# A gather's weighted sums move to TensorE, and two recurrences to VectorE, in a two-layer diffusion trunk

## The chip, the cores and the metric

One core of one Trainium2 chip runs the whole program in one launch. The metric is the device time of one execution in microseconds (us). TensorE multiplies matrices, VectorE and ScalarE work element by element, GpSimd runs small vector operations and issues the indirect DMAs, and SyncE issues the other DMAs. In the rows below they are PE (PEld for its weight loads), DVE, ACT, POOL and SP.

## The reference, cut to what matters

```python
for layer in range(2):                       # latent x: 512 tokens, context xc: 256 tokens, width 1024
    y, yc = token_mixer(h, hc, ...)          # attention + long convolution + S5 scan, gated
    x = x + g1 * y
    x = x + g2 * peer_ffn(modulated norm of x, ...)
    if layer == 0:                           # the context is needed by layer 1 only
        xc = xc + mc[2] * yc
        xc = xc + mc[5] * peer_ffn(modulated norm of xc, ...)

def s5_scan(...):      h[t] = abar * h[t-1] + bu[t]          # complex, forward and backward

def peer_ffn(x, ...):                        # per token: 8 heads x 16 experts of 16384
    expert, gate = top-k of query-key scores
    act = gelu(einsum('btd,bthkd->bthk', x, u_tab[expert]))
    return einsum('bthk,bthkd->btd', gate * act, v_tab[expert])
```

## The kernel before, in words

The program writes its work as generators, called chains here. `weave` (L115 and on) runs several chains at once: each chain has a clock, each `yield` adds its cost (2.6 where none is given) times the chain's factor, and the chain whose clock is lowest goes next. A chain that waits for a mark is held, and its clock is raised to that of the chain that goes on. So a larger factor gives a chain a smaller share, and the factors decide the order in which instructions are written for all engines; each engine then runs its own queue in about that order.

The stages, in time, are these. **Stage A** is layer 0's mixer for latent and context. **Stage B** weaves five chains: layer 0's context mixer (`ctx_rest`), followed at the mark `c1` by `ctx_side` (the context's norm, its scores, and the choice of experts by `pick` for its two tiles of 128 tokens); `peer_u`, which multiplies all 512 latent tokens with 128 slabs of the U table; `side` (from `aside`: S5 and convolution tables for layer 1, the mark `pg`, then the latent's `scores`, four `pick`s and four `table`s of gates, and the mark `tabs`); `gather`; and layer 1's modulation (`mods`). **Stage C** is `peer_v`: 128 slabs of the V table for the latent, while `gather` goes on. **Stage D** is layer 1's mixer; then come layer 1's PEER stages.

`peer_gather` treats a context tile in two rounds of 128 indirect DMAs of 128 rows x 1024 numbers (512 KB each) into the four buffers `gx`. The first round fetches rows of U, and VectorE takes the product with the tokens and its sum (L1198). The second fetches rows of V, and VectorE adds each, weighted, to the result (L170). Round by round it goes tile 0 U, tile 0 V, tile 1 U, tile 1 V. It starts when the experts of a tile are chosen and the buffers `gx` exist; those are opened by `side` after the first `pick` or `table` that ends behind `c1`. In stage B `gather` has the factor 1.69 and ends its turn at `tabs`; the rest runs in stage C with the factor 1.5.

`s5_scan` runs the recurrence of the S5 branch: after `s5_drive` has filled Z (matrix products, copied out by ScalarE at L536), 32 steps for the context and 63 for the latent, four small operations each, on GpSimd, in each layer. `merge` and `merge_lat` gather three gated branches; one addition of each runs on GpSimd.

## Time and profile before

| | us |
|---|---|
| median of 3 runs | 5619.02 |
| lowest, highest | 5601.35, 5627.83 |
| the profiled execution, its own time | 5622.82 |
| its span, first to last instruction | 5621.0 |

Stage boundaries are read from the first and the last instruction on a tile: `pu` belongs to `peer_u` and starts at 973 us, `pa` belongs to `peer_v` and starts at 2572 us, and the chain of layer 1's mixer begins after 3432 us. A row of the view by stretches gives, for each engine, the time in which it was busy and the count of its instructions, and then the clock that TensorE was granted (1.00 is 2.4 GHz, and in each moment it is 1.2 or 2.4), the mean busy share of the 16 DMA engines, and the rate of all transfers. A matmul's recorded time is longer than the spacing of two matmuls, since they are pipelined; the spacing is what a sum of many takes.

### The profile page before, as it was taken

The page shows a single profiled execution, that of the slowest core. Times are in us where ns is not written, and L with a number is a line of the kernel's source. Part 1 is how long each engine was busy: PE and PEld are TensorE (multiplying, and loading weights), DVE is VectorE, ACT ScalarE, POOL GpSimd, SP SyncE. Part 2 cuts the span into 40 slices and gives each one's busy share as a digit, 9 for nine tenths or more (in the row PEclk, how much of TensorE's full clock was granted, in tenths as well). Part 3 has the DMA queues.
Part 4 walks back from the last instruction along what each step waited for, and adds up shares of the span by engine and source line. Part 5 has one row for each costly group of instructions (what it writes and reads, how often), then busy time and mean ns, then how long its engine had stood idle before and what let it go on. Part 6 is the DMA issues. An engine that isn't in the chain of part 4 may idle for free.

```text
span 5621.0 us, 72399 instructions
## 1 busy us (share of the span) xinstructions
PE 4884.9 (87%) x25801; PEld 4022.3 (72%) x25801; DVE 3723.0 (66%) x7594; ACT 1757.1 (31%) x2651; POOL 1480.0 (26%) x1626
## 2 busy tenths in 40 slices
PE   6898878878997889998888887999789899999887
PEld 5676547648986767786676766876578889897775
DVE  5643426654489999995776776544353989877777
ACT  3231514314442222332222223324233333333332
POOL 0003500000002334442444442406000111244443
PEclk8899989889999999999999988999899999999998
DMA  6557335666656889898999997563344576889997
GB/s 206 193 185 260 110 95 187 195 193 195 186 174 200 293 285 321 307 338 311 326 322 308 329 310 243 187 207 101 113 145 153 199 241 233 286 316 322 319 326 267
DMA packets 641793, 1333.38 MB, mean 237 GB/s; under 512 B 56437, under 2 KB 342390, under 8 KB 626328
## 3 DMA queue, kind: packets, MB, share of 16 engines
q1 hardware_dynamic: 522776, 871.53, 47.3%
q0 software_dynamic: 118656, 457.23, 23.0%
q8 instruction: 203, 3.33, 0.2%
q14 instruction: 158, 1.29, 0.1%
HBM read 1147.01 MB, written 181.49 MB: 236 GB/s over the span
## 4 chain that ended last, share of the span: by engine, by line
PE 24%; issue 14%; DVE 12%; DMA 11%; POOL 5%; ACT 1%; SPq 0%; DVEq 0%; POOLq 0%; ACTq 0%
PE pa L181 6%; PE two L181 4%; PE ps L181 4%; PE pu L181 4%; POOL gx L1185 4%; DMA gx<-in_peer_v_dram,t 3%; DVE t L170 2%; DMA gt<-t 2%; PE px L181 2%; PE pf L181 2%; PE pm L181 2%; DVE wl L160 2%; DMA va<-t 1%; DMA t<-ge 1%; DVE xl L160 1%
## 5 line engine op out<-in xcount | busy, mean ns | idle before, releaser
L160 DVE TENSOR_TENSOR wl<-w,wh 128x1024 fp32r<-128x1024 f32 (+1 forms) x550 | 638.9, 1163 | 581.2 <-ACT wh L176 574.7
L176 ACT CAST wh<-w 128x1024 fp32r<-128x1024 f32 (+1 forms) x550 | 545.9, 993 | 1499.9 <-PE pu L181 398.6
L1185 POOL DMA_INDIRECT gx<-in_peer_un_dram,t x384 | 533.3, 1389 | 1595.0 <-DVE t L1198 769.3
L181 PE MATMUL pa<-xl,vwh 128*128 128x512 f32 x1664 | 674.8, 406 | 163.9 <-DVE xl L160 163.7
L1185 POOL DMA_INDIRECT gx<-in_peer_v_dram,t x384 | 592.8, 1544 | 745.3 <-DVE t L170 642.7
L181 PE MATMUL pu<-t,wh 128*128 128x512 f32 x2048 | 661.8, 405 | 31.3 <-ACT ua L173 22.7
L181 PE MATMUL pa<-xh,vwh 128*128 128x512 f32 x1664 | 665.8, 401 | 18.3 <-ACT vwh L176 17.7
L181 PE MATMUL pa<-xh,vwl 128*128 128x512 f32 x1664 | 669.8, 403 | 5.4 <-DVE vwl L160 5.3
L181 PE MATMUL pm<-t,wh 128*128 128x384 f32 (+1 forms) x2432 | 579.4, 324 | 6.9 <-ACT wh L176 6.9
L170 DVE SCALAR_TENSOR_TENSOR t<-gx,t,t 128x1024 f32<-128x1024 f32 x381 | 487.2, 1279 | 52.4 <-DMA gx<-in_peer_v_dram,t 50.8
L181 PEld LDWEIGHTS pa<-xl,vwh 128*128 128x128 f32 x1664 | 324.9, 195 | 248.6 <-DVE xl L160 180.9
L1198 DVE CUSTOM_DVE_ANT_0 gx<-gx,t 128x1024 f32<-128x1024 f32 x384 | 462.6, 1218 | 55.0 <-DMA gx<-in_peer_un_dram,t 54.2
L181 PEld LDWEIGHTS pu<-t,wh 128*128 128x128 f32 x2048 | 391.0, 195 | 114.8 <-ACT ua L173 27.1
L181 PE MATMUL pu<-t,wl 128*128 128x512 f32 x1024 | 415.2, 406 | 57.7 <-DVE wl L160 57.7
L181 PEld LDWEIGHTS pm<-t,wh 128*128 128x128 f32 x2432 | 425.7, 193 | 15.6 <-ACT wh L176 10.0
L181 PE MATMUL pm<-t,wl 128*128 128x384 f32 (+1 forms) x1216 | 393.1, 324 | 34.8 <-DVE wl L160 34.8
L181 PEld LDWEIGHTS pa<-xh,vwh 128*128 128x128 f32 x1664 | 323.7, 195 | 88.5 <-ACT vwh L176 18.6
L181 PEld LDWEIGHTS pa<-xh,vwl 128*128 128x128 f32 x1664 | 325.2, 195 | 76.3 <-DVE vwl L160 8.3
L176 ACT CAST vwh<-gt 128x512 fp32r<-128x512 f32 (+1 forms) x256 | 145.1, 567 | 730.4 <-PE pa L181 589.4
L176 ACT CAST xh<-x 128x1024 fp32r<-128x1024 f32 x256 | 268.5, 1049 | 320.2 <-DMA x<-in_peer_v_dram 269.1
L160 DVE TENSOR_TENSOR gt<-va,gt 128x512 f32<-128x512 f32 (+1 forms) x256 | 152.2, 620 | 289.4 <-DMA gt<-t 205.0
L160 DVE TENSOR_TENSOR xl<-x,xh 128x1024 fp32r<-128x1024 f32 x256 | 311.9, 1218 | 6.3 <-ACT xh L176 6.3
(372 smaller groups left out, 9147.0 us busy)
## 6 DMA issues: line engine op xcount, KB each, us to landing
w<-in_peer_u_dram SPq DMA_DIRECT2D x256, 512.0 KB
x<-in_peer_v_dram SPq DMA_DIRECT2D x256, 512.0 KB
w<-in_in_w_dram SPq DMA_DIRECT2D x128, 512.0 KB
t<-ge SPq DMA_DIRECT2D x56, 1024.0 KB
gt<-t SPq DMA_DIRECT2D x112, 512.0 KB
w<-in_mod_w_dram SPq DMA_DIRECT2D x96, 512.0 KB
dft<-in_dft_dram POOLq DMA_DIRECT2D x32, 1024.0 KB
t<-ua SPq DMA_DIRECT2D x128, 256.0 KB
```

What stands on the lines that cost most here:

```text
L160: return (e or self.nc.vector).tensor_tensor(out=out, in0=a, in1=b, op=op)
L170: self.nc.vector.scalar_tensor_tensor(out=out, in0=a, scalar=s, in1=b, op0=op0, op1=op1)
L176: self.nc.scalar.copy(h, x)
L181: self.nc.tensor.matmul(out, l, r, start=start, stop=stop)
L1185: self.nc.gpsimd.indirect_dma_start(out=g, out_offset=None, in_=src, in_offset=bass.IndirectOffsetOnAxis(ap=ids[:, k:k + 1], axis=0))
L1198: self.nc.vector.tensor_tensor_reduce(out=g, in0=g, in1=x, scale=1.0, scalar=0.0, op0=OP.mult, op1=OP.add, accum_out=dot[:, c:c + 1])
```

## The change

Five edits. The recurrences of `s5_scan` are issued on VectorE, and every step of them yields 1.5 (before, every fourth yielded 0.5). The additions of `merge` and `merge_lat` go to VectorE. For context tile 0 the gather stops after the U round, with the mark `dot`; the V round is done by a new function `summed` at the end of `ctx_side`, in stage B: 128 rows are gathered for 4 tokens x 32 slots at a time and summed by TensorE, with the weights set into a block matrix `z` of 32 columns. `gather` in stage C gets the factor 3.0 in place of 1.5. And `side` gets the factor 1.3 in place of 0.8 until `pg` or `c1`, so 0.6 of its pace beside the context's mixer.

```diff
-        e = nc.gpsimd
+        e = nc.vector
...
-            if i % 4 == 3:
-                yield 0.5
+            yield 1.5
...
-                            self.tt(mf[:, n], mf[:, n], g, OP.add, self.nc.gpsimd)
+                            self.tt(mf[:, n], mf[:, n], g, OP.add)
...
-                                self.tt(mf, mf, g, OP.add, nc.gpsimd)
+                                self.tt(mf, mf, g, OP.add)
...
+    def summed(self, pool, src, ids, w, lane):
...
+        p = self.bank(lane)
+        f = self.t(pool, [128, 128], tag="gi", bufs=1)
+        nc.vector.tensor_copy(f, ids)
+        nc.tensor.transpose(p[:, 0:128], f, self.ident)
+        nc.tensor.transpose(p[:, 128:256], w, self.ident)
+        it = self.t(pool, [128, 128], I32, tag="git", bufs=1)
+        nc.vector.tensor_copy(it, p[:, 0:128])
+        wt = self.t(pool, [128, 4, 32], tag="gi", bufs=1)
+        nc.vector.tensor_copy(wt.rearrange("p g s -> p (g s)"), p[:, 128:256])
+        acc = [self.bank(lane) for _ in range(2)]
+        lag, made = 8 - 4, []
+        for n in range(128 + lag):
+            if n < 128:
+                t = 32 * (n % 4) + n // 4
+                g = self.t(pool, [128, D], tag="gv", bufs=8)
+                nc.gpsimd.indirect_dma_start(out=g, out_offset=None, in_=src,
+                                             in_offset=bass.IndirectOffsetOnAxis(ap=it[:, t:t + 1], axis=0))
+                made.append(g)
+            if n % 4 == (lag - 1) % 4:
+                s = (n - lag - 3) // 4
+                if s >= 0:
+                    if s % 4 == 0:
+                        z = self.t(pool, [128, 4, 4, 32], tag="gz", bufs=2)
+                        nc.vector.memset(z, 0.0)
+                        nc.vector.tensor_copy(z.rearrange("p g s c -> p g (s c)")[:, :, s:s + 100:33], wt[:, :, s:s + 4])
+                    rows = [made.pop(0) for _ in range(4)]
+                    one = lambda c, q: nc.tensor.matmul(acc[c][32 * q:32 * q + 32, :], z[:, q, s % 4, :], rows[q][:, c * 512:(c + 1) * 512],
+                                                        start=s == 0, stop=s == 31)
+                    first = one(0, 3)
+                    with self.tc.issue_after(first.ins):
+                        for c in range(2):
+                            for q in range(3, -1, -1):
+                                if c or q < 3:
+                                    one(c, q)
+                yield 6.4
+        return acc
...
+        if key:
+            self.done.add(key)
+            return
...
+            with self.pool("gv") as gv:
+                yield from until("dot", ("mods", 1))
+                x, w, ids, _ = C[0]
+                acc = yield from self.summed(gv, a["peer_v"].rearrange("l e d -> (l e) d"), ids, w[:, 2].rearrange("p h k -> p (h k)"), "m")
...
-                yield from self.peer_gather(C["gx"], 0, 1, *C[q], c1[q], lambda x: nc.sync.dma_start(c2[q], x))
+                yield from self.peer_gather(C["gx"], 0, 1, *C[q], c1[q], lambda x: nc.sync.dma_start(c2[q], x), None if q else "dot")
...
-                      (part(side, "tables"), lambda: 1.25 if "c1" in self.done else 1.23 if "pg" in self.done else 0.8, "s"),
+                      (part(side, "tables"), lambda: 1.25 if "c1" in self.done else 1.23 if "pg" in self.done else 1.3, "s"),
...
-                    weave((vl, 1.0, "m"), (gather, 1.5, "s"))
+                    weave((vl, 1.0, "m"), (gather, 3.0, "s"))
```

## Rows read from the trace of the kernel before

**Rows 1.** Stretches: us; PE, PEld, DVE, ACT, POOL busy; clock; DMA share; GB/s

```profile
0.00:960.00 960.00, 793.35 (x4594) 593.30 (x4594) 437.34 (x819) 291.47 (x484) 164.96 (x423) 0.90 0.55 176
960.00:1310.00 350.00, 273.88 (x1686) 198.57 (x1685) 203.49 (x467) 108.84 (x189) 4.82 (x9) 0.82 0.66 199
1310.00:1540.00 230.00, 226.72 (x1552) 209.62 (x1551) 95.14 (x123) 95.70 (x135) 16.07 (x19) 1.00 0.58 181
1540.00:1757.00 217.00, 203.60 (x1100) 172.31 (x1099) 188.50 (x746) 88.06 (x133) 0.00 (x0) 0.98 0.56 170
1757.00:2181.00 424.00, 352.99 (x1694) 291.48 (x1692) 392.15 (x1078) 115.49 (x169) 174.21 (x129) 0.92 0.83 293
2181.00:2555.00 374.00, 351.18 (x1753) 294.89 (x1753) 331.41 (x706) 115.52 (x172) 151.71 (x107) 0.97 0.86 308
2555.00:3432.00 877.00, 739.68 (x3063) 598.42 (x3062) 636.61 (x793) 206.85 (x259) 390.85 (x276) 0.91 0.92 320
3432.00:4300.00 868.00, 767.46 (x4305) 603.49 (x4304) 367.87 (x553) 298.94 (x493) 169.62 (x409) 0.93 0.48 154
```

**Rows 2.** Tile `my`, DVE, stage B: count, ns min/median/max, first and last start

```profile
L160 DVE TENSOR_TENSOR my<-pm,rowb x8: 417/420/425, 1499.0 to 1538.1; 128x256 f32<-128x256 f32 x8
```

**Rows 3.** Tile `gx`, 1497 to 3432 us: the first gathers of U and of V

```profile
L1185 POOL DMA_INDIRECT gx<-in_peer_un_dram,t x256: 939/1165/1996, 1757.4 to 3047.6; - x128
...
L1185 POOL DMA_INDIRECT gx<-in_peer_v_dram,t x255: 939/1154/4094, 2180.6 to 3431.7; - x128
```

**Rows 4.** Groups by line, DVE, 1757 to 2555 us: count | busy us, mean ns | idle before

```profile
L1198 DVE CUSTOM_DVE_ANT_0 gx<-gx,t 128x1024 f32<-128x1024 f32 x128 | 154.5, 1215 | 19.2 <-DMA gx<-in_peer_un_dram,t 19.1
...
L170 DVE SCALAR_TENSOR_TENSOR t<-gx,t,t 128x1024 f32<-128x1024 f32 x102 | 130.3, 1277 | 8.0 <-DMA gx<-in_peer_v_dram,t 7.4
```

**Rows 5.** DMA view, 1757 to 2555 us: bytes, and issues with count and size

```profile
DMA packets 69163, 239.47 MB, mean 300 GB/s; under 512 B 7680, under 2 KB 7680, under 8 KB 65013
...
w<-in_peer_u_dram SPq DMA_DIRECT2D x96, 512.0 KB
...
t<-ua SPq DMA_DIRECT2D x101, 256.0 KB
...
gx<-in_peer_un_dram,t POOLq DMA_INDIRECT x128
gx<-in_peer_v_dram,t POOLq DMA_INDIRECT x107
```

**Rows 6.** DMA view, stage C, 2555 to 3432 us

```profile
DMA packets 143552, 280.53 MB, mean 320 GB/s; under 512 B 9567, under 2 KB 75103, under 8 KB 143505
...
gx<-in_peer_v_dram,t POOLq DMA_INDIRECT x148
```

**Rows 7.** Waits of stage C: engine, line, releaser: us, times, longest

```profile
ACT xh L176 <- DMA x<-in_peer_v_dram: 167.9, 48, 13.2
DVE gt L160 <- DMA gt<-t: 129.7, 12, 12.2
...
PE pa L181 <- DVE xl L160: 115.0, 19, 10.3
```

**Rows 8.** Timeline, PE, stage C: start, length, instruction

```profile
2806.81 0.39 PE L181 MATMUL pa<-xh,vwh 128*128 128x512 f32 x1
2807.03 0.39 PE L181 MATMUL pa<-xl,vwh 128*128 128x512 f32 x1
2807.26 0.39 PE L181 MATMUL pa<-xh,vwl 128*128 128x512 f32 x1
```

**Rows 9.** Groups by line and shape, whole span, PE: 32-column products of `mods`

```profile
L181 PE MATMUL pm<-w,t 128*32 128x256 f32 x384 | 41.4, 439 | 6.9 <-DMA w<-in_mod_w_dram 6.4 <-DVE my L160 0.5
```

**Rows 10.** Groups by line, whole span, POOL: the recurrence's second and third operation

```profile
L160 POOL TENSOR_TENSOR ch_q<-t,t 128x64 f32<-128x64 f32 x190 | 79.1, 416 | 0.0
...
L160 POOL TENSOR_TENSOR ch_p<-ch_p,t 128x64 f32<-128x64 f32 x190 | 69.7, 367 | 182.3 <-ACT t L536 182.2
```

**Rows 11.** Groups by line and shape, whole span, DVE: the nearest operation in size

```profile
L160 DVE TENSOR_TENSOR off<-pf,off 128x64 f32<-128x64 f32 x20 | 4.4, 218 | 0.2
```

**Rows 12.** Tile `ch_p`, 540 to 800 us: the latent's recurrence, first and last start

```profile
L160 POOL TENSOR_TENSOR t<-ch_p,ch_q x64: 317/320/1372, 540.3 to 713.7; 128x64 f32<-128x64 f32 x64
```

**Rows 13.** Tile `PT`, 540 to 800 us: the latent's attention beside it

```profile
L885 DVE COPY PT<-two x18: 676/692/692, 596.9 to 759.3; 128x512 f32<-128x512 f32 x18
```

More of the change, by code (lines that the diff above doesn't have):

```diff
@@ L1191, in gathered, with peer_gather @@
             yield 1.6
-    def peer_gather(self, pool, l, j, x, p, ids, dot, src, put):
+    def summed(self, pool, src, ids, w, lane):
+        nc = self.nc
+        p = self.bank(lane)
[34 more added lines that the diff above has]
+        return acc
+    def peer_gather(self, pool, l, j, x, p, ids, dot, src, put, key=None):
         w = p[:, 2].rearrange("p h k -> p (h k)")
@@ L1516, in ctx_side @@
                 self.done.add(("ids", q))
+            with self.pool("gv") as gv:
+                yield from until("dot", ("mods", 1))
+                x, w, ids, _ = C[0]
+                acc = yield from self.summed(gv, a["peer_v"].rearrange("l e d -> (l e) d"), ids, w[:, 2].rearrange("p h k -> p (h k)"), "m")
+                g = self.rows(gv, 0, 1, 5, "gv", 8)
+                y = self.t(gv, [128, D], tag="gv", bufs=8)
+                nc.sync.dma_start(y, c1[0])
+                for c in range(2):
+                    k = slice(c * 512, c * 512 + 512)
+                    self.tt(x[:, k], acc[c], g[:, k], OP.mult)
+                self.tt(x, x, y, OP.add)
+                nc.sync.dma_start(c2[0], x)
         def gather():
@@ L1529, in run @@
                       (chain(until("h"), self.peer_u(0, ua, hs[0], TL, lambda i: act[i], "tabs"), mark("u")), lambda: 1.2 if "c1" in self.done else 10.0, "u"),
-                      (part(side, "tables"), lambda: 1.25 if "c1" in self.done else 1.23 if "pg" in self.done else 0.8, "s"),
-                      (self.while_(gather, "tabs"), 1.69, "s"), (mods(1, range(6), 0, 1), 1.26, "m"))
-            self.done.add(("mods", 1))
+                      (part(side, "tables"), lambda: 1.25 if "c1" in self.done else 1.23 if "pg" in self.done else 1.3, "s"),
+                      (self.while_(gather, "tabs"), 1.69, "s"), (chain(mods(1, range(6), 0, 1), mark(("mods", 1))), 1.26, "m"))
             with self.pool("pv", True) as pv:
```

## The prediction, made before the change was run

> **What bounds the kernel now.** I read the view by stretches first, then the DMA view of the two stretches in which the context's gather runs, then the waits of stage C. In stage A and again in stage D TensorE is busy for 0.83 and 0.88 of the time, while VectorE is busy for less than half, GpSimd for a fifth, and transfers run at 176 and 154 GB/s [rows 1]: the reader sees TensorE-bound work with idle helpers. From 1310 to 1540 us, the context's merge, TensorE is busy for 226.7 of 230 us at the full clock: that stretch has no slack, and work taken out of it shortens it. The context mixer's output is finished with the last of its eight `my` operations at 1538 us [rows 2], so the mark `c1` lies at about 1540 us. Then 217 us of scores and expert choices follow, until the first gather at 1757 us [rows 3].
>
> From there to the end of stage C three things are nearly full at once. VectorE is busy for 392.2 + 331.4 = 723.6 of 798 us (0.907) up to 2555 us, and transfers run at 293 and 308 GB/s; in stage C they run at 320 GB/s with the DMA engines busy for 0.92, the highest stretch of the table [rows 1]. The waits of stage C say who is late there: ScalarE waits 167.9 us for the V slabs and VectorE 129.7 us for the gates, both from DMA, and TensorE's own 115.0 us come behind VectorE, which waits for the same slabs through ScalarE [rows 7]. So stage C is bound by transfers: 280.5 MB [rows 6]. The question for the change is thus less which engine sums than **when the gather can start and which stage carries its bytes**.
>
> **The weave, counted.** I counted the chains' clocks from the yields and factors of the code; the unit is the weave's, and no time is taken from it. Before: `side` passes `pg` at 210 and has 12 of its 16 score steps behind it when `c1` comes at 298; the gather starts at 450; `tabs` comes at 1078, `peer_u` ends at 1099; 233 gathers lie in stage B and 283 turns (with the lag's) in C. The trace agrees: 128 + 107 gathers before 2555 us [rows 5], and after it 148 of V [rows 6] and 128 of U, the second half of the 256 of [rows 3]. After: at `c1` (298) `side` is still in the convolution tables, with all 16 score steps and the last 12 of 34 table steps to come; `ctx_side` is held for `pg` until 339; the buffers `gx` open after the first `pick`, at 540, and the gather starts there. U of tile 0 ends at 888, `summed` runs from 888 to 1121 beside U of tile 1, `peer_u` ends at 1112, and `tabs` comes at 1208. Stage B then has 248 gathers through VectorE (129 + 119) and 128 for `summed`; stage C has 138 in place of 276.
>
> **The change part by part.**
>
> *Up to c1.* Twelve score steps leave. Each is 24 matmuls of 512 columns, spaced 0.227 us [rows 8], so 5.44 us, 65 us in all, out of stretches of which the main one is full. The 12 table steps hold 4 x 24 matmuls of half the columns, some 12 us by half that spacing. Less company in the first 350 us, where TensorE runs at a clock of 0.82 and waits on short chains [rows 1], may give another 10. I take **-87 us**, with bounds -60 (that work sat in gaps) and -120. The additions that move off GpSimd cost VectorE 16 operations of about 0.4 us in a stage where it is busy for half the time; nothing.
>
> *From c1 to the first gather.* The same 12 scores and 12 table steps come back here (65 + 12), and the chosen factors put 31 `peer_u` slabs ahead of the gather where there were 18: 13 x 5.44 = 71 us. That is 148 us more for TensorE, which is busy for 203.6 of 217 us there already [rows 1]. At that share, 148 / 0.94 = 158; I take **+160 us**. The lower bound is +90 (the slabs run under the expert choices, which need VectorE alone), the upper +200 (the choices wait for all the scores, so they stand behind them). Together with the part above the first gather is at 1757 - 87 + 160 = 1830 us.
>
> *From the first gather to stage C.* VectorE's sum hardly moves: it loses 104 weighted additions at 1277 ns and gains 119 products at 1215 ns [rows 4], some +12 us; `summed` itself costs it 8 clears and 8 small copies, under 10 us, and 13 slabs less to split take about as much off. What grows is transfer: 376 gathers in place of 235, 141 x 0.524 MB = 73.9 MB more, less 13 slabs at 0.786 MB (512 + 256 KB, [rows 5]) = 10 MB. So 239.5 + 64 = 303 MB. At stage C's 320 GB/s that is 947 us; at the 300 GB/s of the stretch itself 1010 us. Since in the section 540 to 888 VectorE is the limit and only behind it both streams of gathers run at once, I take a value between, 965 us, **+167 us** over 798. If VectorE were the limit throughout it would be (723.6 + 12) / 0.907 = 811, +13: that is the lower bound, and 1010 with no further loss the upper one, +212.
>
> The rows show 320 GB/s as the most that a stage of this kernel moved [rows 1]. The Trainium skill ("DMA: Bandwidth & Descriptors", "Specifications") gives some 358 GB/s as what HBM yields to one core; no stretch of the table reaches it. By that figure the 303 MB would take 846 us, an estimate, and the sum below would be 119 us less.
>
> TensorE's sums: 32 steps x 2 halves x 4 = 256 products of 32 columns by 512. `mods` has the same kind with 256 columns: 384 records, two for each product, in 41.4 us [rows 9], where four run side by side. With 512 columns, 512 records of twice that length are 110 us; records that follow closely could halve it. In this stretch TensorE is idle for 798 - 353.0 - 351.2 = 94 us [rows 1], 13 slabs less free 71 more, and the transfers make it longer: this idle time hides the sums, so I cost them at nothing, and at up to +110 if the slabs have to wait behind them. What is queued behind a sum that waits for its rows is the next slab of `peer_u` on TensorE, and behind that the splits on VectorE. GpSimd's queue has both streams in order: a gather for `gx` waits for VectorE's product four gathers back, and the rows for `summed` stand behind it.
>
> *Stage C.* It loses 138 gathers x 0.524 = 72 MB, and as many products and additions on VectorE. 208 MB at 320 GB/s are 651 us, below TensorE's need: 128 slabs x 24 x 0.227 = 697 us. So TensorE becomes the limit, with some 20 us at the ends and a remainder of the stalls. The 180 us over 697 are those ends, TensorE's idle time (877 - 739.7 = 137 us) and the lower clock (0.91, [rows 1]); I leave the ends and about a third of the rest: 775 us, **-102 us**. The floor is 717 (-160); two thirds of the rest kept give 822 (-55).
>
> *Stages A and D.* Four operations a step move: 2 x 95 steps x 4 x about 0.21 us [rows 11] = 160 us for VectorE, 80 in each stage, where it is busy for 437 of 960 and 368 of 868 us [rows 1]. On GpSimd they took about 0.4 us each [rows 10] and were ahead of need: the latent's recurrence ended at 714 us, the attention beside it at 760 us [rows 12, 13], and the new yields let the last step end with the attention (391 against 394 in A, 280 against 279 in D). The added wait is the one for ScalarE's copies of Z, on which GpSimd stood 182.2 us in four waits [rows 10]; on VectorE the splits of the next weights and the attention's maxima queue behind it. With three buffers for split weights VectorE is no more than about three weight tiles ahead of TensorE, so a wait is a few us. I take **+10 us** for both, from -20 (the convolution's DMA issues no longer queue behind the recurrence on GpSimd) to +40.
>
> The sum: -87 + 160 + 167 - 102 + 10 = +148. The profiled execution took 5622.8 us, 0.07% over the median, so no correction is made: 5771, **5770 us**.
>
> **The rivals.**
>
> *Transfers keep up (faster).* If VectorE alone limits the stretch with the gathers, so that 303 MB pass in 811 us, and stage C falls to its floor of 717 us, then -87 + 160 + 13 - 160 + 10 = -64: 5559 us. For it: VectorE is at 0.907 there and its sum is the same. Against it: 303 MB in 811 us are 374 GB/s, and no stretch of [rows 1] is over 320. It becomes a gain where the 303 MB pass in under 875 us, at over 346 GB/s.
>
> The page of the Trainium skill named above, "DMA: Bandwidth & Descriptors", stands on this rival's side: with its 358 GB/s and stage C's floor the total would be an estimated 5594 us.
>
> *The average rate holds.* The bytes from the first gather to the end of stage C are 520 MB before, in 1675 us: 310 GB/s. After they are 303 + 208 = 511 MB. If that average held over both stages, TensorE's floor in C notwithstanding, they take 1648 us from 1830 us on: an end at 3478 in place of 3432, and with A and D 5679 us. The same comes out if the pace does nothing, because the engines run `side`'s scores in the merge as before: then -87 + 160 drop out, and 167 - 102 + 10 = +75, 5698 us. So 5600 to 5700.
>
> *TensorE's queue is held.* The sums wait in line for their rows and hold the slabs behind them: +110 us on the forecast, 5880 us. For it: 31 groups of sums in a section where transfers are the limit.
>
> **How the numbers follow.** Forecast (5700 to 5840): 0.60. Average rate or no effect of the pace (5600 to 5700, mostly slower, a third of it within 28 us of before): 0.18. Faster: 0.12. Queue held: 0.10. About 0.5%, 28 us, is what a measurement of this kernel can tell from no change. So faster 0.13, same 0.08, slower 0.79. The range is 5610 to 5890: it takes in the middle cases and the held queue, and leaves out the faster one and the far end, some 0.2.
>
> **What would show it.** `c1` (the last `my<-pm`) some 90 us earlier; the first gather not earlier than before, near 1830 us; over 300 MB between it and the first `pa`, at 305 to 325 GB/s; `pa` from some 2800 us on; stage C 80 to 130 us shorter with a rate below 290 GB/s and fewer waits for slabs. A first gather before 1757 us, or a rate over 340 GB/s beside the sums, would make the prediction wrong.

## The result, and the profile after

| | before | after |
|---|---|---|
| median of 4 runs each, on one chip, us | 5620.21 | 5655.09 |
| lowest, highest | 5601.35, 5627.83 | 5654.84, 5655.92 |
| span of the profiled execution | 5621.0 | 5653.1 |

The changed kernel takes 1.0067 of the time of the kernel before, with a 95% interval of 1.0042 to 1.0092: slower by 35 us. The forecast was slower by 148 us, with a range of 5610 to 5890.

Marks near those of the forecast come from the first and last starts on `my`, `gx` and `pa`. They cut both profiled executions into stretches:

| us | before | after | difference | forecast |
|---|---|---|---|---|
| start to the end of stage A | 939 | 938 | -1 | |
| to `c1` (last `my`) | 599 | 505 | -94 | -87 |
| `c1` to the first product on gathered rows | 228 | 385 | +157 | +160 |
| first product to the first `pa` | 806 | 925 | +119 | +167 |
| stage C, first to last `pa` | 862 | 716 | -146 | -102 |
| the rest | 2187 | 2184 | -3 | +10 (with A) |
| sum | 5621 | 5653 | +32 | +148 |

The view by stretches of the kernel after, with the columns of [rows 1]:

```profile
0.00:965.00 965.00, 803.52 (x4640) 600.09 (x4640) 502.84 (x1219) 295.70 (x497) 15.45 (x32) 0.89 0.56 177
...
1310.00:1444.00 134.00, 128.72 (x958) 120.90 (x957) 83.34 (x137) 62.69 (x87) 2.64 (x5) 0.97 0.75 238
1444.00:1828.00 384.00, 361.26 (x1845) 301.12 (x1844) 207.22 (x769) 129.72 (x192) 5.07 (x6) 0.97 0.52 158
1828.00:2262.00 434.00, 385.96 (x1825) 317.66 (x1824) 411.49 (x1079) 128.28 (x183) 174.55 (x133) 0.95 0.86 300
2262.00:2665.00 403.00, 334.15 (x1832) 235.44 (x1830) 281.81 (x742) 88.26 (x135) 238.36 (x207) 0.92 0.98 384
2665.00:2754.00 89.00, 22.77 (x81) 16.06 (x73) 60.25 (x116) 7.30 (x12) 42.85 (x37) 0.54 0.89 306
2754.00:3454.00 700.00, 690.36 (x3001) 565.46 (x3001) 467.61 (x529) 199.33 (x254) 220.65 (x134) 0.99 0.87 289
3454.00:4330.00 876.00, 779.73 (x4350) 609.89 (x4349) 426.45 (x941) 299.61 (x493) 8.52 (x16) 0.93 0.47 149
```

Three rows matter. From 2262 to 2665 us, where `summed` fetches its rows, transfers run at 384 GB/s with the DMA engines busy for 0.98; no stretch of [rows 1] was over 320. Right behind it lie 89 us in which TensorE is busy for 22.8 and its clock is granted at 0.54, so mostly at the lower of its two levels. And stage C has become TensorE's: busy for 690 of 700 us at 0.99, against 739.7 of 877 at 0.91 in [rows 1].

The tiles of the marks in the same execution (count, ns least/median/most, first and last start), to be held against [rows 2] and [rows 3]:

```profile
L160 DVE TENSOR_TENSOR my<-pm,rowb x8: 414/418/424, 1420.4 to 1443.4; 128x256 f32<-128x256 f32 x8
L1184 POOL DMA_INDIRECT gx<-in_peer_un_dram,t x256: 932/1099/2283, 1793.2 to 2774.8; - x128
L1212 POOL DMA_INDIRECT gv<-in_peer_v_dram,git x128: 932/940/3683, 2263.7 to 2638.0; - x128
```

The context mixer is done 95 us earlier and the gather still starts 36 us later than in [rows 3]; its first product starts 62 us later (1828 against 1766). The forecast's own mark was the first gather. In the kernel after, GpSimd issues that one alone (start, length, queue and, in brackets, the idle time before):

```profile
1793.16 1.00 POOL L1184 DMA_INDIRECT gx<-in_peer_un_dram,t  x1 [319.67 <-DVE pf L1084]
1825.22 1.44 POOL L1184 DMA_INDIRECT gx<-in_peer_un_dram,t  x1 [31.05 <-DVE i L1055]
```

The second gather comes 31 us behind it; before, 0.3 us of idle time lay between the two. So the table counts by the first product. By the first gather the two differences around it would be +131 and +146 us in place of +157 and +119, with the same sum.

The V-slab products, which bound stage C, kernel before, then kernel after:

```profile
L181 PE MATMUL pa<-xh,vwh x896: 387/389/796, 2571.6 to 3433.3; 128*128 128x512 f32 x180
```

```profile
L181 PE MATMUL pa<-xh,vwh x896: 387/389/796, 2753.7 to 3468.9; 128*128 128x512 f32 x180
```

The waits of stage C in the kernel after, 2754 to 3454 us (engine, tile and line, releaser: us, times, longest), against [rows 7]:

```profile
DVE gt L160 <- DMA gt<-t: 119.5, 14, 10.8
PEld pa L181 <- DVE xl L160: 16.5, 20, 4.1
...
ACT xh L176 <- DMA x<-in_peer_v_dram: 12.9, 12, 3.9
```

ScalarE's wait for V slabs has fallen from 167.9 us to 12.9. VectorE's wait for gates, which the prediction read as a sign of what limits stage C, has hardly fallen (129.7 us before), so it did not set the length of the stage.

**The tail ahead of stage C.** Stage C begins when the chains of stage B are done, `peer_u` and the gate tables (`tabs`) among them. The last `pu` of the larger group starts at 2554.6 us before and at 2593.9 us after; the last product of the tables (`ps`) at 2538.6 us before, ahead of it, and at 2727.0 us after, long behind it. The two groups, kernel before, then kernel after:

```profile
L181 PE MATMUL pu<-t,wh x556: 387/389/628, 2301.3 to 2554.6; 128*128 128x512 f32 x186
L181 PE MATMUL ps<-ohB,ohA x880: 270/275/582, 1904.1 to 2538.6; 128*128 128x128 f32 x176
```

```profile
L181 PE MATMUL pu<-t,wh x512: 387/389/796, 2300.9 to 2593.9; 128*128 128x512 f32 x171
L181 PE MATMUL ps<-ohB,ohA x1024: 270/275/583, 1937.9 to 2727.0; 128*128 128x128 f32 x171
```

The view by stretches from the last `pu` to the first `pa`, kernel before, then kernel after:

```profile
2554.60:2571.60 17.00, 0.64 (x3) 0.19 (x1) 1.39 (x2) 2.30 (x4) 0.00 (x0) 0.58 0.84 257
```

```profile
2593.90:2753.70 159.80, 65.98 (x332) 48.57 (x330) 109.11 (x249) 20.00 (x35) 69.99 (x64) 0.62 0.88 312
```

Before, 17 us pass between them. After, 160: the U slabs are used up, the last tables and sums are all that TensorE has, and it is busy for 66 us of it. Counted from the end, 143 of the 182 us by which stage C begins later are this tail; counted from the start, 62 of them are there at the first product. These are two views of one delay and are not to be added. The chain that ended last shows what the tables stand behind (start, length, piece):

```profile
2668.72 7.91 DMA gx<-in_peer_un_dram,t
2676.76 1.23 DVE gx L1239
...
2682.25 5.61 DMA gx<-in_peer_un_dram,t
2687.99 1.23 DVE gx L1239
```

The tables' small operations share VectorE's queue with the products on gathered rows, and several of those wait for their rows.

### The profile page after: what moved, and what is told of

The parts are those of the page before. It is cut to its first block, busy times and chain, and to the rows that moved or that the text cites. A ratio compares the mean times of both kernels' runs of the same rounds, so it can differ in the third digit from the quotient of the medians.

```text
span 5653.1 us, 73111 instructions
## 1 busy us (share of the span) xinstructions
PE 4947.9 (88%) x26315; PEld 4026.7 (71%) x26315; DVE 3706.1 (66%) x8284; ACT 1756.3 (31%) x2652; POOL 1115.3 (20%) x828
## 4 chain that ended last, share of the span: by engine, by line
PE 35%; DVE 13%; DMA 13%; issue 10%; ACT 1%; POOL 1%; SPq 1%; DVEq 0%; ACTq 0%; POOLq 0%
PE pa L181 13%; PE ps L181 5%; PE pm L181 4%; PE two L181 4%; PE px L181 3%; DMA gt<-t 3%; PE pu L181 3%; DMA gv<-in_peer_v_dram,git 2%; DMA gx<-in_peer_un_dram,t 2%; DVE wl L160 2%; DVE gx L1239 2%; PE pf L181 1%; DMA va<-t 1%; DMA t<-ge 1%; DVE t L170 1%
## 5 line engine op out<-in xcount | busy, mean ns | idle before, releaser
L1184 POOL DMA_INDIRECT gx<-in_peer_un_dram,t x384 | 503.9, 1312 | 1943.4 <-PE pm L181 689.4
L181 PE MATMUL pa<-xl,vwh 128*128 128x512 f32 x1664 | 661.4, 398 | 56.5 <-DVE xl L160 56.4
L181 PE MATMUL pa<-xh,vwh 128*128 128x512 f32 x1664 | 656.7, 395 | 26.2 <-ACT vwh L176 26.2
L181 PE MATMUL pa<-xh,vwl 128*128 128x512 f32 x1664 | 658.3, 396 | 0.7 <-DVE vwl L160 0.7
L1184 POOL DMA_INDIRECT gx<-in_peer_v_dram,t x256 | 435.5, 1701 | 711.5 <-DVE t L170 642.4
L181 PE MATMUL ps<-ohB,ohA 128*128 128x128 f32 x1792 | 264.9, 297 | 106.8 <-ACT ge L1140 55.6
L675 POOL DMA_DIRECT2D dft<-in_dft_dram x38 | 20.6, 542 | 1703.9 <-DVE wl L160 496.6
L181 PEld LDWEIGHTS ps<-ohB,ohA 128*128 128x128 f32 x1792 | 244.5, 206 | 138.9 <-ACT ge L1140 66.5
```

The costliest lines, as they stand in the source:

```text
L181: self.nc.tensor.matmul(out, l, r, start=start, stop=stop)
L675: self.nc.gpsimd.dma_start(c, self.a[f"dft{T}"][fc])
L1184: self.nc.gpsimd.indirect_dma_start(out=g, out_offset=None, in_=src, in_offset=bass.IndirectOffsetOnAxis(ap=ids[:, k:k + 1], axis=0))
```

## The experiments

Times are medians, and each ratio is to the kernel before on the same chip, whose median there was between 5602.4 and 5609.6 us. Marks and rows come from one execution of each run, and executions of one kernel differ by up to 41 us: the profiled one was 20 us above the median in the run with the pace by itself, 18 below it in the run without the sums, and within 9 us of it in all others but one (13 below, the first with `side` faster).

### The pace by itself

```diff
-  (part(side, "tables"), lambda: 1.25 if "c1" in self.done else 1.23 if "pg" in self.done else 0.8, "s"),
+  (part(side, "tables"), lambda: 1.25 if "c1" in self.done else 1.23 if "pg" in self.done else 1.3, "s"),
```

> The kernel before with the pace of the side chain alone (factor 1.3 in place of 0.8). My theory, that the pace moves twelve score steps from the full merge stretch to the stretch between c1 and the first gather, where they come at 157 us against 95 us won: c1 some 95 us earlier, the first gather some 60 us later, total +50 to +70 us. Rival, that the pace pays for itself once the gather is spread as before: within 15 us of before.

5679.19 us, 1.0123 [1.0094, 1.0153]: 69 us slower than before. `c1` comes at 1462 us (76 earlier) and the first product at 1848 (82 later); stage C is 859 us, as before. The stretch between the last `pu` and the first `pa`, with the columns of [rows 1]:

```profile
2553.10:2666.30 113.20, 55.95 (x252) 48.95 (x250) 88.46 (x180) 20.02 (x35) 52.08 (x34) 0.58 0.82 271
```

The pace alone opens the tail, without any sum: 113 us, TensorE busy for 56 of them. `peer_u` ends when it did (2553 against 2554.6 us), and the tables that were put off end last. The first `pa` comes 95 us later than before, and the tail is 96 us longer: in this run the tail holds the whole delay of stage C.

### The recurrences and additions on VectorE by themselves

```diff
-        e = nc.gpsimd
+        e = nc.vector
...
-            if i % 4 == 3:
-                yield 0.5
+            yield 1.5
...
-    self.tt(mf, mf, g, OP.add, nc.gpsimd)
+    self.tt(mf, mf, g, OP.add)
```

> The kernel before with the recurrences and the merge additions on VectorE alone. My theory: they were off the path and stay near it, +5 to +15 us in stages A and D together. Rival, that GpSimd's operations held VectorE's up (two SBUF inputs on either side): 10 us or more faster.

5620.48 us, 1.0020 [1.0005, 1.0035]: 3 to 20 us slower. The row of the operation that [rows 10] has on GpSimd (busy, mean ns, idle before), from the groups by line:

```profile
L160 DVE TENSOR_TENSOR ch_p<-ch_p,t 128x64 f32<-128x64 f32 x190 | 41.6, 219 | 13.3 <-ACT t L535 13.2
```

One operation takes 219 ns where GpSimd took 367, and VectorE waits 13.2 us for ScalarE where GpSimd had waited 182.2. Both are far from the end of their stages: no mark moves by more than some 8 us.

### The change with the old pace

```diff
-  (part(side, "tables"), lambda: 1.25 if "c1" in self.done else 1.23 if "pg" in self.done else 1.3, "s"),
+  (part(side, "tables"), lambda: 1.25 if "c1" in self.done else 1.23 if "pg" in self.done else 0.8, "s"),
```

> The changed kernel with the old pace (0.8 in place of 1.3), so the sums on TensorE, the recurrences on VectorE and the halved share of the gather in stage C are kept. My theory: it wins back the 60 us that the pace costs before the first gather, so about 5595 us, 25 us faster than before (1.0067 falls to about 0.996). Rival, that the pace is needed for the balance of stages B and C: 5640 us or more.

5565.68 us, 0.9932 [0.9907, 0.9957]: 44 us faster than the kernel before, and by its median the fastest of the kernels here that leave nothing out. Its tail, then all of the time from 960 us to the first `pa`:

```profile
2648.90:2665.40 16.50, 0.66 (x3) 0.20 (x2) 1.39 (x2) 2.30 (x4) 0.00 (x0) 0.65 0.82 248
...
960.00:2665.00 1705.00, 1471.07 (x8236) 1171.42 (x8236) 1217.48 (x3246) 513.81 (x774) 458.19 (x375) 0.93 0.77 269
```

The tail is back at 16.5 us. The same long stretch of the kernel after and of the kernel before:

```profile
960.00:2754.00 1794.00, 1501.74 (x8279) 1193.07 (x8271) 1241.40 (x3287) 528.18 (x799) 465.58 (x390) 0.91 0.75 261
```

```profile
960.00:2572.00 1612.00, 1408.99 (x7779) 1167.15 (x7777) 1212.47 (x3119) 526.31 (x800) 346.80 (x263) 0.93 0.73 243
```

TensorE is idle for 1612 - 1409 = 203 us before, 234 with the old pace, and 292 in the kernel after. So the sums add 62 us of busy time and 31 of idle time, and the pace adds 58 us of idle time and 31 of busy time, the latter for nearly the same work (8279 matmul records against 8236, the clock at 0.91 in place of 0.93). These differences are good to some 10 us, since stage A's end differs by so much between the executions. With either pace, stage C gains: 705 us here, 716 after. And the transfers beside the sums are faster still than in the kernel after, 403 GB/s over 374 us:

```profile
2196.00:2570.00 374.00, 339.86 (x1854) 237.21 (x1853) 271.19 (x667) 91.28 (x135) 237.62 (x205) 0.96 1.01 403
```

### Stage C with little work for VectorE

In the kernel before, for the second context tile alone:

```diff
+            g, x = (g[:, 0:32], xx[:, 0:32]) if few else (g, xx)
...
-                self.stt(x, g, w[:, c:c + 1], x, OP.mult, OP.add)
+                y, g = (xx[:, 0:32], g[:, 0:32]) if few else (xx, g)
+                self.stt(y, g, w[:, c:c + 1], y, OP.mult, OP.add)
```

> The kernel before, with the products and weighted additions of context tile 1 (its U and V rounds, which lie in stage C) taken on 32 of 1024 columns; every gather is kept. That part of the computation is changed. If transfers set stage C's 860 us from the first to the last V-slab product, it stays within 30 us of that. If VectorE's queue sets it, it falls towards the floor of 697 us, to 760 or less.

5586.51 us, 0.9963 [0.9944, 0.9982]; stage C takes 844 us, 18 less. Stage C in the view by stretches, and then one of its waits:

```profile
2562.00:3406.00 844.00, 743.06 (x3068) 599.18 (x3069) 389.28 (x799) 205.22 (x256) 342.68 (x277) 0.94 0.95 330
```

```profile
PE pa L181 <- DVE xl L160: 97.4, 33, 9.4
```

VectorE is busy for 389 us in place of 637, and TensorE waits almost as long for the split slabs as in [rows 7] (115.0), with the DMA engines at 0.95. With all the bytes left in, VectorE's relief is worth 18 us, although it shortens 255 operations to a thirty-second of their columns, where the change takes 138 away.

### Stage C with fewer gathers

In the kernel before, for the second context tile, with `every` = 2 in one kernel and 8 in the other; VectorE's work stays:

```diff
-                g = self.t(pool, [128, D], tag="gx", bufs=4)
-                self.nc.gpsimd.indirect_dma_start(out=g, ...)
+                if k % every == 0:
+                  g = self.t(pool, [128, D], tag="gx", bufs=4)
+                  self.nc.gpsimd.indirect_dma_start(out=g, ...)
```

> The kernel before, with one gather in two for context tile 1, its rows used twice; VectorE's products and additions are all kept. That part of the computation is changed. This takes 128 gathers out of stage C, about as many as the change does (138). If their transfers alone made the change's stage C short (716 us from the first to the last V-slab product, 862 before), it comes to 710 to 740 here. If the relief of VectorE had a part in it, it stays at 770 or more.

> The kernel before, with one gather in eight for context tile 1, its rows used eight times; VectorE's products and additions are all kept. That part of the computation is changed. If transfers set stage C, its 860 us fall to about 700 to 720 (224 gathers less). If VectorE's queue sets it, 820 us or more stay.

With half of the gathers: 5524.48 us, 0.9861 [0.9831, 0.9892], stage C 774 us. With an eighth: 5461.22 us, 0.9748 [0.9715, 0.9781], stage C 729 us. Stage C by stretches and then the same wait, first with half of the gathers, then with an eighth:

```profile
2568.00:3342.00 774.00, 725.56 (x3067) 588.55 (x3068) 635.63 (x801) 203.85 (x257) 215.28 (x149) 0.97 0.84 274
```

```profile
PE pa L181 <- DVE xl L160: 42.0, 20, 5.5
```

```profile
2551.00:3280.00 729.00, 710.09 (x3066) 577.74 (x3067) 634.29 (x801) 202.03 (x256) 73.41 (x53) 0.99 0.71 223
```

```profile
PE pa L181 <- DVE xl L160: 13.6, 14, 2.5
```

128 gathers are worth 88 us of stage C, 0.69 us each, and their bytes alone bring it to 774 (two executions were measured, one is shown). The change takes 138 gathers and their operations on VectorE away and comes to 716. That leaves 51 us (774 - 716, less ten gathers at 0.69) for VectorE's relief and for the larger factor, which spreads the gathers over the stage in another way; these two runs do not divide it. With an eighth of the gathers and VectorE as busy as before (634 us), the stage is 32 us above the 697 of TensorE's need: once few transfers stand beside it, VectorE's work can cost no more than that.

### The sums without TensorE

In the kernel after, the gathers of `summed` stay and all but two groups of its products go:

```diff
+                    if s % 31:
+                        nc.scalar.copy(z[:, 0, 0, 0:4], rows[3][:, 0:4])
+                        yield 6.4
+                        continue
                     one = lambda c, q: nc.tensor.matmul(acc[c][32 * q:32 * q + 32, :], ...)
```

> The changed kernel with TensorE's sums of summed left out but for the first and the last group of 32, the 128 gathers kept. That part of the computation is left out. My theory, that the sums lie in TensorE's idle time and transfers set the stretch from the first product to the first V-slab product (926 us): within 20 us of it. Rival, that the sums hold the slabs behind them in TensorE's queue: 50 us or more shorter.

5623.55 us, 1.0035 [1.0019, 1.0051]. From the first product to the first `pa` it takes 867 us in place of 925: by this one execution the sums cost 58 us there, as the rival theory said. Of the whole kernel the medians show less, 1.0067 - 1.0035, some 18 us, and the two intervals overlap. The edit also puts a small copy on ScalarE for each group left out, and those wait 40.8 us for the rows, so it takes the products away and not every wait for their rows. What they are in the kernel after, from the groups by line on TensorE, 2262 to 2665 us:

```profile
L1223 PE MATMUL pm<-gv,gz 128*32 128x512 f32 x512 | 67.3, 647 | 30.9 <-DMA gv<-in_peer_v_dram,git 30.8
```

67 us busy and 31 us waiting for rows at the head of TensorE's queue. Without them the stretch from 960 us to the first `pa` is 76 us shorter (some 11 of them because stage A ended earlier in this execution), and TensorE is idle for as long as in the kernel after (288 and 292 us):

```profile
960.00:2678.00 1718.00, 1429.69 (x7754) 1178.75 (x7754) 1205.83 (x3232) 523.18 (x808) 446.62 (x367) 0.91 0.76 264
```

So idle time elsewhere did not take the sums in here. Not all of the 58 us reach the end: stage C takes 746 us here, 30 more than in the kernel after, with TensorE waiting 51.2 us for V slabs behind ScalarE at six points, where the kernel after waits 26.2 us at one. Why stage C is longer without the sums stays open.

### The sums with a quarter of the rows

```diff
-                g = self.t(pool, [128, D], tag="gv", bufs=8)
-                nc.gpsimd.indirect_dma_start(out=g, ...)
+                if n % 4 == 0:
+                  g = self.t(pool, [128, D], tag="gv", bufs=8)
+                  nc.gpsimd.indirect_dma_start(out=g, ...)
```

> The changed kernel, with one gather in four for the sums of summed, its rows used four times; all sums are kept. That part of the computation is changed. If transfers set the 925 us from the first product to the first V-slab product, 96 gathers less at 1.3 us each shorten it by up to 120 us, to about 830, and less where VectorE takes over. If TensorE's queue alone sets it, it stays within 25 us.

5567.31 us, 0.9929 [0.9901, 0.9957]. The stretch takes 850 us, 75 less than in the kernel after, for 96 gathers: 0.78 us each. Of the 75 us, 55 are the tail:

```profile
2575.70:2680.20 104.50, 56.78 (x284) 48.63 (x282) 80.96 (x202) 19.80 (x35) 33.35 (x28) 0.62 0.79 267
```

The whole kernel shows the same, 1.0067 - 0.9929, some 77 us. So the rows have a price that medians show, and the products one of 58 us in one execution. The two overlap (75 + 58 is more than the 119 us by which the stretch grew, and a sum whose rows are there does not wait either); neither transfers alone nor TensorE's queue alone explains the 119 us.

### The sums and their share alone

The kernel after with the pace at 0.8, and recurrences and additions back on GpSimd:

```diff
-        e = nc.vector
+        e = nc.gpsimd
...
-            yield 1.5
+            if i % 4 == 3:
+                yield 0.5
```

> The kernel before with the sums of tile 0 on TensorE and the halved share of the gather in stage C, and nothing else of the change (old pace, recurrences and additions on GpSimd). My theory, that the parts add: the run without the pace was 44 us faster than before and the recurrences cost 11, so some 50 us faster than before (ratio 0.990 to 0.992). Rival, that the sums gain only with VectorE's recurrences: ratio 0.995 or more.

5569.72 us, 0.9949 [0.9931, 0.9967], between the two expectations. Its marks are those of the change with the old pace (first `pa` at 2665.1 and 2665.4 us, stage C 705 us in both), and the intervals overlap. Beside the sums, moving the recurrences has no effect that these runs can tell.

### A denser gather in stage C

The change with the old pace, and the gather's factor in stage C at 2.6:

```diff
-                    weave((vl, 1.0, "m"), (gather, 3.0, "s"))
+                    weave((vl, 1.0, "m"), (gather, 2.6, "s"))
```

> The changed kernel with the old pace (0.8) and the factor 2.6 in place of 3.0 for the gather in stage C, where 154 gathers are left by the count of the weave: at 3.0 they take 740 units beside the slabs' 674, at 2.6 they take 641. My theory: as fast as the run with the old pace or up to 15 us faster (5550 to 5566 us), since the last gathers no longer follow the slabs. Rival: a denser gather slows the slabs again, 10 us or more slower than that run.

5586.31 us, 0.9969 [0.9955, 0.9984], against 0.9932 [0.9907, 0.9957] with 3.0: some 20 us slower, though the intervals touch. Two waits of stage C:

```profile
DVE gt L160 <- DMA gt<-t: 129.9, 14, 10.8
...
PE pa L181 <- DVE xl L160: 24.7, 18, 2.6
```

Stage C takes 736 us in place of 705, and TensorE waits for split slabs again, 24.7 us against 4.4 in the same wait with 3.0. The expectation, as fast or faster, failed. The thinner gather is part of what brought the stage to TensorE's floor: 31 us here lie in the factor alone.

### The pace the other way

Sums and share alone, with `side` faster beside the context's mixer, and the gather's factor in stage C at 2.5 (the second kernel also gives the context's chain more room behind `c1`):

```diff
-  (part(side, "tables"), lambda: 1.25 if "c1" in self.done else 1.23 if "pg" in self.done else 0.8, "s"),
+  (part(side, "tables"), lambda: 1.4 if "c1" in self.done else 0.9 if "pg" in self.done else 0.6, "s"),
```

```diff
-  (chain(self.ctx_rest(...), mark("c1"), ctx_side()), lambda: 1.1 if "c1" in self.done else 1.0, "m"),
+  (chain(self.ctx_rest(...), mark("c1"), ctx_side()), lambda: 0.7 if "c1" in self.done else 1.0, "m"),
...
+  (part(side, "tables"), lambda: 1.45 if "c1" in self.done else 0.9 if "pg" in self.done else 0.6, "s"),
```

> The kernel with the sums only, and the side chain faster beside the context's mixer (0.6 until pg, 0.9 until c1, then 1.4; gather 2.5 in stage C): the reverse of the change's pace. My theory, that scores and expert choices cost less in the merge, where VectorE is idle for over half the time, than between c1 and the first gather: c1 20 to 40 us later, the stretch to the first product 60 us or more shorter, so 15 to 40 us faster than with the sums only. Rival, that the old pace is the best place: no faster than the sums only.

> As the run with the faster side chain, and the context's own scores and choices after c1 ahead of the U slabs (0.7 in place of 1.1; the side chain 1.45 then). My theory: the first gather comes some 30 us earlier still, and with transfers at 413 GB/s at most the whole gains as much. Rival: the slabs pushed behind it are missed later, no gain over that run.

5632.44 us, 1.0061 [1.0039, 1.0082], and 5683.22 us, 1.0149 [1.0125, 1.0172]. In the first, `c1` comes 83 us later than with 0.8, and what follows it gives back 10 us (218 in place of 228), so the first product comes at 1826 us, as late as with 1.3. The view by stretches on both sides of `c1`:

```profile
1310.00:1608.00 298.00, 280.04 (x1772) 250.42 (x1771) 142.02 (x365) 119.16 (x168) 16.45 (x17) 0.96 0.52 159
1608.00:1826.00 218.00, 196.57 (x1109) 166.93 (x1107) 174.93 (x612) 86.17 (x136) 5.66 (x4) 0.95 0.55 175
```

TensorE is busy for 0.94 and 0.90 of the time, so the side ahead of `c1` had no room for the work pulled there. In the second, the first product comes 36 us earlier than in the first (1790), about as expected, but from there to the first `pa` it takes 977 us in place of 883: the rival, slabs that are missed later, fits. Of the three paces tried, 0.8 is the best. The first kernel loses 63 us to sums and share alone, but not all of it to the pace: stage C takes 738 us in place of 705, about as with the factor 2.6 above.

## Why the sign was right and the size wrong, step by step

**The weave count was right.** `c1` came 95 us earlier (87 forecast), and then 157 us more passed to the first product (160 forecast, to the first gather). The slower pace of `side` moves the scores and tables behind `c1` and U slabs ahead of the gather, as counted.

**What the count said of the end was not used.** It put the end of `peer_u` at 1112 and `tabs` at 1208, where before it was 1099 and 1078. So it said that tables would outlast the slabs, and the step "From the first gather to stage C" took from it only how many gathers lie where. The tail is that order, measured: 17 us before, 113 with the pace alone, 160 in the kernel after, 16.5 with the old pace. The pace costs 69 us by itself, and between the kernel after and the one with the old pace 1.0067 - 0.9932, some 75 us. The forecast had this price, -87 + 160 = +73, at the other end: the first product comes 77 us later than with the old pace (1828 against 1751), and the first `pa` 88. So the tail is where the late gather shows, not a second loss. Whether the tables end last because they start late or because they queue behind the products, these runs do not separate. Of the whole change the pace is the part that loses; the rest gains 44 us.

**The transfers were priced too high; here the sum failed first.** The step "From the first gather to stage C" took 303 MB at 314 GB/s, from stage C's 320 as the most that a stage moved, and got 965 us, 167 more than before; by the marks used here that is 806 + 167 = 973. The stretch moved 337 x 0.926 = 312 MB in 925 us, and without the sums 346 x 0.867 = 300 MB in 867 us. Stage C's 320 GB/s were no ceiling. A rate over 340 GB/s beside the sums was the prediction's own sign of being wrong, and it came. In the kernel after, the DMA view from 2262 to 2665 us (rate in 40 slices; packets by size; queue: packets, MB, share of 16 engines):

```profile
GB/s 393 418 263 393 417 412 409 410 365 336 243 375 414 416 413 410 410 415 412 414 414 412 413 414 412 419 411 410 419 414 413 416 410 415 407 278 348 343 136 303
DMA packets 43106, 154.65 MB, mean 384 GB/s; under 512 B 4793, under 2 KB 4793, under 8 KB 41135
...
q0 software_dynamic: 29942, 109.02, 69.3%
q1 hardware_dynamic: 13138, 45.30, 28.3%
```

and stage C of the kernel before, 2572 to 3432 us, whose packets stand in [rows 6]:

```profile
q1 hardware_dynamic: 99081, 132.06, 47.6%
q0 software_dynamic: 39361, 143.35, 44.7%
```

In stage C half of the packets are under 2 KB [rows 6]; here 4793 of 43106 are, and slices reach 410 to 419 GB/s. In the stage itself the gathers' queue moves 143.35 MB in 44.7% of 860 us, 373 GB/s of the engines' time, and the other 132.06 MB in 47.6%, 323. So a gather of 0.524 MB takes an estimated 1.4 us of the engines, not the 1.64 that the stage's mean gives. The rows of the kernel after agree: 109.02 MB in 69.3% of 403 us are 390 GB/s, 1.34 us a gather. What one gather less saved in time was about half of that, 0.69 us in stage C and 0.78 in the stretch. The rival "transfers keep up" had its turning point at 346 GB/s, on the ground that no row was over 320; the queues' own shares, which the trace of before has too, give a reason to doubt that ground.

The Trainium skill ("DMA: Bandwidth & Descriptors", "Specifications") gives some 358 GB/s as what HBM yields to one core. This kernel, a program on one core, moved 384 GB/s over 403 us, so the figure was no bound for it. The same page of the Trainium skill says under "Measured" that about 358 is what each core gets when both cores of a pair stream; the prediction took it for what one core gets in any case. What the pair's other core did, no run here shows.

**The sums were not free.** The step costed them at nothing because of 94 + 71 us of idle TensorE time in the stretch. In the one execution without their products the stretch was 58 us shorter, close to their 67 us of busy time, and with the old pace TensorE's busy time up to stage C is 62 us more than before while its idle time grows too: the idle time did not take them in. Of the whole kernel their price is smaller and not clear of noise, some 18 us. The rival "TensorE's queue is held" was right in kind; its +110 was about twice the price, since the 512 records were busy for 67 us. This miss hid part of the other, by luck: without the sums the error of the stretch would have been 106 us, not 48.

**Stage C came close to its floor; here the sum failed a second time.** The step "Stage C" kept about a third of the stalls, -102 us: 775 of the 877 us in its rows, 760 of the 862 from the first to the last `pa`. Half of the gathers with VectorE as it was gives 774, -88 us, and by the same price the 138 gathers are -95, so for the bytes alone the step was about right. It counted "as many products and additions on VectorE" and gave their relief no price, nor the gather's larger factor. Together these hold up to 51 us more: VectorE's relief is worth 18 us alone, and the step of the factor from 3.0 to 2.6 cost 31 with the old pace; how they divide the 51 is not shown. So the stage took 716 us in place of 760, with TensorE busy for 0.99 of it.

**Stages A and D.** +10 forecast, -4 on the profiles, and +3 to +20 us for that edit by itself: small, as said.

In sum: the weave's part was forecast at +73 and came to +63 (the two marks around `c1`), the exchange between the gather's stretch and stage C was forecast at 167 - 102 = +65 and came to 119 - 146 = -27. The sign was right because of the first, the size wrong because of the second, whose sign came out the other way. The rival "no effect of the pace" expected +75 from that exchange; the run with the old pace shows -44.

The rival "the average rate holds" came nearest, with 5679 us in all and 3478 for the end of stage C, measured 5655 and 3469. Its number was luck: from the first product to the last `pa` the kernel after moved 516 MB at 314 GB/s, but with half of stage C's gathers left out it is 453 MB at 286, and with a quarter of the rows of `summed` 466 MB at 298. An average that falls with the bytes does not set the time.

## What to carry to other kernels

Price a transfer by the share of the DMA engines' time that its own queue takes for its bytes, not by the rate of the stage in which it is seen (this is a price in the engines' time; in two runs here half of it was saved in time); a stage's best rate is a ceiling only where its packets are like those to be moved. When an edit relieves two resources that are late together, and spreads one of them as well, do not add the single prices up: 88 us for the bytes and 18 for VectorE by themselves stand against 146 for the change, in which the spread has a part. And when work is put off in an interleaved stage, ask which chain is last at its end: a tail in which only the put-off chain is left costs TensorE its time and its clock.

## What the hardware did that was not expected

- One core moved 384 GB/s over 403 us with 512 KB gathers as most of its bytes, in long stretches 410 to 419, and 403 over 374 us with the old pace, where stage C, with half of its packets under 2 KB, had 320 to 330 at a DMA share of 0.92 to 0.95.
- In the four long tails (104 to 160 us) TensorE was busy for 0.35 to 0.54 of the time and its granted clock was 0.58 to 0.64; in the 700 us of stage C behind the longest it was busy for 0.99 and the clock was 0.99.
- The recurrences' third operation took 219 ns on VectorE against 367 on GpSimd [rows 10], and moving 760 such operations brought no gain: 1.0020 [1.0005, 1.0035].
